# A decoder layer with attention and DeltaNet heads: the second half's x on GpSimd's queue, squares as stationary in the norm sums, a residual that is loaded later

## The chip, the cores and the metric

One core of a Trainium2 chip runs the whole kernel. The metric is the device time of one execution in microseconds (us). The engines are TensorE (PE; its weight loads are PEld), VectorE (DVE), ScalarE (ACT), GpSimd (POOL) and SyncE (SP). SP computes nothing here: it only issues transfers. ACT and POOL issue transfers too, each on a queue of its own, between their own instructions.

## The reference, cut to what matters

One layer, batch 1, 1024 positions, width 1024, all in float32:

```
u    = RMSNorm(x)
proj = u @ w_in            # attn q|k|v, dn q|k|v, dn z gate, dn beta, dn a
A    = sliding-window attention with sinks (8 heads, 2 kv heads, window 128)
qc, kc, vc = silu(causal_conv(dn q|k|v))
qc   = qc * rsqrt(sum(qc*qc) + eps) * 128**-0.5      # l2norm per row and head
kc   = kc * rsqrt(sum(kc*kc) + eps)
B    = chunked gated delta rule over 16 chunks of 64, a scan with a 128x128 state
       per head (4 heads), then a gated RMSNorm
h    = x + concat(A, B) @ w_o
h   += relu(RMSNorm(h) @ w_up)**2 @ w_down
h   += sigmoid(RMSNorm(h) @ w_ple_gate) * (p @ w_ple_proj)
out  = RMSNorm(h)
```

The changed code sits in three places: the loading of x for RMSNorm, the sums of squares for the two l2norms, and the x in `h = x + ...`.

## The kernel before, in words

The positions are worked on in two halves (`hb` 0 and 1) of 512. Every float32 product of a weight is made of three passes of float32r matmuls (high with high, high with low, low with high; `PASSES`), so a weight is loaded, cast on ACT (L219) and its low part subtracted on DVE or POOL (L220) before TensorE can use it. All matmuls have the line L102, the line of a helper, so the names of the tiles say which is which: `bk<-w,U` and `bk<-U,w` are projections of the first half, `bk<-R,w`, `bk<-w,R` those of the second, `bk<-w,AT` the early product `p @ w_ple_proj`, `bk<-vn,ka` a step of the DeltaNet scan, `bk<-rD,wide` a sum of squares. In this trace the second name of a pair is the moving operand in some rows and the stationary in others; the shape at the end of a row is that of the moving side.

The text of the kernel is not the order in which it runs. A class `Flow` runs generators against an invented clock: the DeltaNet and attention chains are tasks that yield times, and the big products (`projections`, `embed`, `w_out`) are a filler that gives TensorE work whenever no task is due. Behind it a scheduler of the framework orders the instructions of each engine by its own model. So an edit in one place can change the order of instructions far from it. On the chip each engine then takes its list in order and waits at an instruction whose inputs are not there, with everything that stands behind it.

The names in the order of time:

- `u_step(hb, ...)` (L347 to L358) loads the eight 128x512 pieces of xT of one half (256 KB each, L351), scales and splits each into high and low parts for the first projection (ACT, DVE), squares it (ACT) and adds it up (`eng`, here POOL, L358). The second half has only four slots (`AT`) for its eight pieces, and the sum `rsb` is the first of them.
- `wunit2` (L278 to L285) loads two k tiles of a weight on SP's queue (L281) into one of two `raw` buffers.
- `scalars`, `norms`, `pre`, `inverse` (L627 to L784) prepare the DeltaNet half: `norms` makes the sums of squares of q and k for each row and head, `pre` the products k*k and k*q with their decay (`ka`, L751) and writes blocks of them to DRAM (`LD`, L757, SP's queue); `inverse` reads them back into `rD` (L770, SP), multiplies (L775, DVE) and solves a small triangular system on DVE (L779, L780).
- `merge`, `prep`, `scan` finish the inverse for each 128 rows and run the recurrent scan.
- `embed` (L1049 to L1079) is spare filler: `p @ w_ple_proj`, copied out of PSUM by ACT (L1072) and stored to DRAM (`PD`, L1075, SP).
- `w_out(hb)` (L1004 to L1045) loads x of that half once more as the residual (L1006, two transfers of 1 MB on ACT's queue, into `H` and for the second half also `AT`), multiplies by w_o and adds on DVE.

Of the kernel before, what the change touches and what calls it, by code (L numbers as in the profile page):

```python
# [12 lines left out]
AF = mybir.ActivationFunctionType  # L13
ALU = mybir.AluOpType
# [4 lines left out]
P = 128  # L19
# [4 lines left out]
HB = 512  # L24
FF = 4096
EPS = 1e-6
# [92 lines left out]
def hybrid_block(ctx, tc, t, out):  # L119
    nc = tc.nc  # L120
    V, A, G, SY = nc.vector, nc.scalar, nc.gpsimd, nc.sync
    flow = Flow()
    T = Pe(tc, flow)
    cnt = [0]

    def nm(s):
        cnt[0] += 1
        return f"{s}{cnt[0]}"
# [13 lines left out]
    def bank(p):  # L142
        return p.tile([P, 512], F32, tag="b", name=nm("bk"))
# [13 lines left out]
    def take(k):  # L157

        live = ring[k]
        while live.n == 0:  # L160
            yield live
        live.n -= 1
        b = bank(ps[k])

        def free():
            live.n += 1
        return b, free

    def ctile(shape, name, dt=F32):
        return cp.tile(shape, dt, tag=name, name=name)  # L170
# [13 lines left out]
    ident = con[:, K_ID:K_ID + P]  # L184
    mle = con[:, K_LE:K_LE + P]
    onesR = ctile([P, P], "ones", F32R)
    ones = onesR.bitcast(F32)
# [56 lines left out]
    def uview(u, b, kt):  # L244
        o = (b * KT + kt) * HB
        return u[:, o:o + HB]
# [31 lines left out]
    def wunit2(src, k2, c0, lo_eng=None, n=256):  # L278

        raw = wraw.tile([P, WN], F32, tag="raw", name=nm("raw"))[:, :2 * n]  # L280
        SY.dma_start(raw.rearrange("p (k n) -> p k n", k=2),  # L281
                     src.rearrange("(k p) n -> p k n", p=P)[:, k2 * 2:k2 * 2 + 2, c0:c0 + n])
        w = wsp.tile([P, 2, WN], F32R, tag="w", name=nm("w"))[:, :, :2 * n]
        split(w[:, 0], w[:, 1], raw, lo_eng or G)
        return w  # L285
# [57 lines left out]
    def slot(n):  # L343
        return AT[n // 4][:, n % 4 * HB:(n % 4 + 1) * HB]


    def u_step(hb, u, eng):  # L347
        def step(kt):
            acc = rsb[hb]
            xr = slot(4 * hb + kt % (4 if hb else 8)) if kt else acc  # L350
            SY.dma_start(xr, t["xT"][kt * P:(kt + 1) * P, hb * HB:(hb + 1) * HB])  # L351
            g = gmix[:, kt:kt + 1]
            A.activation(uview(u, 0, kt), xr, AF.Copy, scale=g)
            V.scalar_tensor_tensor(uview(u, 1, kt), xr, g, uview(u, 0, kt).bitcast(F32),
                                   op0=ALU.mult, op1=ALU.subtract)
            A.activation(xr, xr, AF.Square)
            if kt:
                eng.tensor_tensor(acc, acc, xr, op=ALU.add)  # L358
        return step
# [253 lines left out]
    def dt_(shape, name, p=dn, bufs=None, dt=F32):  # L613
        return p.tile(shape, dt, tag=name, name=nm(name), bufs=bufs)
# [2 lines left out]

    dn0 = zs.rearrange("p t (h s) -> p t h s", h=4)
    dn1 = []

    wide = ctile([P, 2 * P], "wide")
    G.memset(wide, 0.0)
    G.memset(wide[:, P:P + 1], 1.0)
    sel = lambda c: wide[:, P - c:2 * P - c]
    offL = con[:, K_OFF:K_OFF + 64]

    def scalars(s, hb):  # L627
# [42 lines left out]
    def norms(s, q, k):  # L670

        b, free = yield from take("e")
        sq = dt_([P, 2, 4, P], "rD", bufs=1, dt=F32R).bitcast(F32).rearrange("p i h c -> p i (h c)")
        xs = [(sel(h * 32 + i), x[:, h, 3:]) for i, x in enumerate((q, k)) for h in range(4)]
        for j in range(9):
            if j < 8:
                A.activation(sq[:, j % 2], xs[j][1], AF.Square)
                yield 0.99
            if j:
                T.matmul(b, xs[j - 1][0], sq[:, (j - 1) % 2], start=j == 1, stop=j == 8)  # L680
        sb = dt_([P, 4, P], "et", bufs=1).rearrange("p h c -> p (h c)")
        A.copy(sb, b)
        free()
        yield 2.38
        b, free = yield from take("e")
        for tt in range(4):
            T.transpose(b[:, tt * P:(tt + 1) * P], sb[:, tt * P:(tt + 1) * P], ident)
        for i in range(2):
            V.tensor_scalar(s["ss"][:, i].rearrange("p (t h) -> p t h", t=4),
                            b.rearrange("p (t h x) -> p x t h", t=4, h=4)[:, i], EPS, None,  # L690
                            op0=ALU.add)
        free()
        w = lambda name: dt_([P, 16], name, bufs=2)
        rk2, rk, c2d, cc, bb = w("rk2"), w("rk"), w("c2d"), w("cc"), w("bb")
        ssq, ssk = s["ss"][:, 0], s["ss"][:, 1]
        V.reciprocal(rk2, ssk)
        V.tensor_tensor(bb, s["beta"], rk2, op=ALU.mult)
        yield 3.17
        b, free = yield from take("e")
        T.transpose(b[0:16, 0:P], bb, ident)  # L700
        bT = dt_([16, P], "bT", bufs=1)
        A.copy(bT, b[0:16, 0:P])
        free()
        SY.dma_start(s["BD"], bT)
        bS = dt_([P, 32], "bS")
        for x in range(2):
            SY.dma_start(bS[x * 64:x * 64 + 64], s["BD"].rearrange("y (b c) -> (y b) c", b=4))
        G.tensor_tensor(rk, ssk, mhalf, op=ALU.pow)
        sc4 = dt_([P, 4, 2, 2, 2], "sc4", bufs=2)
        v = lambda x: x.rearrange("p (t g h) -> p t g h", t=4, g=2)  # L710
        V.tensor_tensor(sc4[:, :, :, 0], v(bb), v(s["eG"]), op=ALU.mult)
        V.tensor_tensor(sc4[:, :, :, 1], v(s["beta"]), v(rk), op=ALU.mult)
        V.reciprocal(c2d, ssq)
        V.tensor_scalar(c2d, c2d, 1.0 / (128.0 * 128.0), None, op0=ALU.mult)
        G.tensor_tensor(cc, ssq, mhalf, op=ALU.pow)
        V.tensor_scalar(cc, cc, 128.0 ** -0.5, None, op0=ALU.mult)
        s.update(bb=bb, bS=bS, sc4=sc4, c2d=c2d, cc=cc)
# [281 lines left out]
    def hT(hb, j, n=1):  # L999

        x, o = (H, XW + j * HB) if hb == 0 else (H, j * HB) if j < 4 else (AT[1], (j - 4) * HB)
        return x[:, o:o + n * HB]

    def w_out(hb):  # L1004
        for j in (0, 4):
            A.dma_start(hT(hb, j, 4).rearrange("p (j s) -> p j s", j=4),  # L1006
                        t["xT"].rearrange("(j p) s -> p j s", p=P)[:, j:j + 4, hb * HB:hb * HB + HB])

        def rhs(b, kt):
            return dn1[b][:, kt - 4] if hb and kt > 3 else uview(R1, b, kt)  # L1010

        def steps(g, bs, ks):
            for kt in ks:
                if kt % 2 == 0:
                    w = wunit2(t["w_o"], kt // 2, g * 256, (G, G)[hb])
                for m in range(2):
                    o = kt % 2 * 256 + m * P
                    (mm3h, mm3h)[hb](bs[m][0], lambda a: w[:, a, o:o + P], lambda b: rhs(b, kt), kt == 0, kt == KT - 1)
                    if kt < KT - 1 or m == 0:
                        yield  # L1020
            if kt == KT - 1:
                for m in range(2):
                    h = hT(hb, g * 2 + m)
                    V.tensor_tensor(h, bs[m][0], h, op=ALU.add)
                    bs[m][1]()
                yield

        early = ["gg", "ge", "ee"] if hb else []
        held = []
        for g, names in enumerate(early):  # L1030
            if "e" in names:
                yield prepped
            bs = []
            for k in names:
                bs.append((yield from take(k)))
            yield from steps(g, bs, range(4))
            held.append(bs)
        if hb:
            yield pairs_done[1]
        for g in range(4):  # L1040
            if g < len(held):
                yield from steps(g, held[g], range(4, KT))
                continue
            bs = []
            for k in "gg":  # L1045
                bs.append((yield from take(k)))
            yield from steps(g, bs, range(KT))
# [37 lines left out]
    def projections():  # L1085
# [37 lines left out]
        dn1.extend(h4(part(x, F32R)) for x in ("AT0", "Z"))  # L1123
        mixed.done = True
        yield from w_out(0)
        mix_split(1, 0)
        yield from w_out(1)


    b = bank(ps["e"])  # L1130
# [288 lines left out]
    for n in range(16):  # L1419
        q = qs[n].load() if n < 4 else Quad(n).load()  # L1420
# [21 lines left out]
    def bank2():  # L1442
        par[0] = (par[0] + 1) % 8
        return bank(ps["gygygywy"[par[0]]])
# [5 lines left out]
    for c in range(FF // 512):  # L1450
# [13 lines left out]
        for nh in range(2):  # L1464
            wd = []
            for hb in range(2):
# [9 lines left out]
                for m in range(4):  # L1476
                    h = hT(hb, nh * 4 + m)
# [4 lines left out]
    for kt in range(KT):  # L1482
        for nh in range(2):
            i = kt * 2 + nh
# [11 lines left out]
    for tt in range(NT):  # L1496

        nT = mpart().rearrange("p (b k s) -> p b k s", b=2, k=KT)
        hb, ts = tt // 4, slice(tt % 4 * P, tt % 4 * P + P)
        hs_ = [hT(hb, j, 4).rearrange("p (j s) -> p j s", j=4)[:, :, ts] for j in (0, 4)]  # L1500
        hv, c2, cg, c = hn[:, tt % 2 * D:(tt % 2 + 1) * D], ba[:, tt, 0:2], ba[:, tt, 2:3], ba[:, tt, 3:4]
# [3 lines left out]
        for q in range(2):  # L1505
            b = bank2()
# [99 lines left out]
```

## Time and profile before

| | us |
|---|---|
| median of 3 runs | 1371.62 |
| the three runs | 1372.47, 1365.68, 1371.62 |
| the profiled execution's own time | 1366.2 |
| its span in the trace | 1364.1 |
| TensorE busy (share of the span) | 1317.7 (97%) |
| VectorE busy | 838.8 (61%) |
| ScalarE busy | 548.0 (40%) |
| GpSimd busy | 434.5 (32%) |
| mean granted TensorE clock | 0.987 |

The profiled execution is one execution; 2.1 us of its time lie outside the span. Busy time is the time in which an engine works on an instruction; the granted clock is a share of full speed, so a stretch at 0.60 holds fewer columns than its busy time suggests. The kernel's instructions are pipelined on TensorE, so its busy time holds short waits between matmuls as well.

### The profile page before, as it was taken

Reading aid. Unit: us, or ns where it says so; the run is one execution under the profiler, and the core shown is the slowest. Engines: PE = TensorE matmul, PEld = TensorE weight load, DVE = VectorE, ACT = ScalarE, POOL = GpSimd, SP = SyncE. Lnnn points to the kernel's source line nnn. Section 1 sums busy time; section 2 is a strip of 40 time slices with the busy share of each in tenths; the row PEclk is TensorE's granted clock in tenths of the full one; section 3 lists DMA queues with packets and bytes.
Section 4 is the critical chain, followed back from the end, with each engine's and each line's share of the span. In section 5 each row is a group of like instructions: output and inputs, shape, how many; then the busy total and the mean of one; then the engine's idle time right before and its main releaser. Section 6 shows DMA issues by size and latency. Waiting matters only on the chain.

```text
span 1364.1 us, 20392 instructions
## 1 busy us (share of the span) xinstructions
PE 1317.7 (97%) x7664; PEld 1125.5 (83%) x7664; DVE 838.8 (61%) x1558; ACT 548.0 (40%) x1083; POOL 434.5 (32%) x430
## 2 busy tenths in 40 slices
PE   8999999999998999898999999999999999999997
PEld 6788688999897998886788888877888888888886
DVE  6786977697564755797776676654333343344553
ACT  6456375544544433564333333342122231221333
POOL 6673626631385452300011111103122212210332
PEclk9999999999999999999999999999999999999999
DMA  6322222324135431321433323354333333232211
GB/s 223 88 54 73 54 62 52 74 73 105 34 119 176 133 110 33 115 85 63 146 116 116 124 87 114 109 185 136 96 116 101 98 123 120 77 93 73 75 62 47
DMA packets 102738, 134.33 MB, mean 98 GB/s; under 512 B 16400, under 2 KB 71744, under 8 KB 102384
## 3 DMA queue, kind: packets, MB, share of 16 engines
q1 hardware_dynamic: 90528, 110.50, 27.0%
q10 hardware_dynamic: 11760, 21.77, 4.4%
q8 instruction: 60, 0.98, 0.3%
q0 software_dynamic: 352, 0.76, 0.2%
q14 instruction: 38, 0.31, 0.1%
HBM read 106.77 MB, written 26.23 MB: 98 GB/s over the span
## 4 chain that ended last, share of the span: by engine, by line
PE 74%; DVE 11%; DMA 6%; ACT 3%; issue 3%; POOL 2%; SPq 1%; POOLq 0%; ACTq 0%; DVEq 0%
PE bk L102 72%; PE bk L106 2%; DVE w L220 1%; DVE cv L412 1%; DMA AD<-t 1%; ACT w L219 1%; DMA raw<-in_w_in 1%; POOL rsb L358 1%; DMA PD<-po 1%; DMA raw<-in_w_down 1%; DMA H<-in_w_in 1%; DMA AT<-in_xT 0%; DVE gg L649 0%; DMA raw<-AD 0%; SPq L841 0%
## 5 line engine op out<-in xcount | busy, mean ns | idle before, releaser
L102 PE MATMUL bk<-T,w 128*128 128x512 f32 x2304 | 537.9, 392 | 5.7 <-ACT w L219 4.5
L102 PEld LDWEIGHTS bk<-T,w 128*128 128x128 f32 x2304 | 432.8, 188 | 102.6 <-ACT w L219 6.6
L220 POOL TENSOR_TENSOR w<-raw,w 128x512 fp32r<-128x512 f32 x136 | 180.5, 1329 | 621.3 <-ACT w L219 590.2
L219 ACT CAST w<-raw 128x512 fp32r<-128x512 f32 (+1 forms) x280 | 172.6, 620 | 460.8 <-PE bk L102 340.6
L102 PE MATMUL bk<-R,w 128*128 128x256 f32 (+1 forms) x1536 | 240.7, 312 | 1.4 <-ACT w L219 1.4
L102 PEld LDWEIGHTS bk<-R,w 128*128 128x128 f32 x1536 | 210.8, 189 | 22.9 <-issue 2.3
L220 DVE TENSOR_TENSOR w<-raw,w 128x512 fp32r<-128x512 f32 (+1 forms) x144 | 107.5, 748 | 61.1 <-ACT w L219 60.9
L1478 DVE TENSOR_TENSOR H<-bk,H 128x512 f32<-128x512 f32 x96 | 64.6, 690 | 96.0 <-PE bk L102 96.0
L102 PE MATMUL bk<-U,w 128*128 128x512 f32 (+1 forms) x384 | 80.3, 355 | 1.0 <-ACT ba L472 0.6
L102 PEld LDWEIGHTS bk<-U,w 128*128 128x128 f32 x384 | 60.2, 191 | 14.5 <-issue 4.9
L102 PE MATMUL bk<-w,R 128*128 128x256 f32 (+1 forms) x480 | 69.4, 294 | 0.1
L102 PE MATMUL bk<-w,U 128*128 128x256 f32 (+2 forms) x384 | 64.1, 321 | 5.2 <-ACT AT L478 3.2
L102 PE MATMUL bk<-AT,w 128*128 128x256 f32 (+1 forms) x256 | 65.3, 342 | 1.3 <-DVE t L1363 0.8
L102 PEld LDWEIGHTS bk<-w,U 128*128 128x128 f32 x384 | 55.6, 194 | 12.3 <-ACT AT L478 3.4
L102 PEld LDWEIGHTS bk<-w,R 128*128 128x128 f32 x480 | 61.7, 192 | 4.0 <-issue 3.1
L1348 ACT ACTIVATE t<-t 128x512 f32<-128x512 f32 x64 | 40.3, 631 | 39.1 <-DVE t L1347 38.4
L102 PEld LDWEIGHTS bk<-AT,w 128*128 128x128 f32 x256 | 42.8, 191 | 8.3 <-DVE t L1363 1.9
L102 PE MATMUL bk<-R,T 128*128 128x512 f32 (+1 forms) x204 | 48.7, 386 | 0.0
L220 POOL TENSOR_TENSOR T<-ra,T 128x1024 fp32r<-128x1024 f32 x14 | 33.6, 2398 | 46.7 <-ACT T L219 41.0
L102 PE MATMUL bk<-T,T 128*128 128x512 f32 (+1 forms) x204 | 47.0, 379 | 0.0
L555 ACT ACTIVATE s<-s,mx 128x257 f32<-128x257 f32 (+1 forms) x64 | 31.3, 492 | 36.8 <-DVE mx L553 30.2
L102 PEld LDWEIGHTS bk<-T,T 128*128 128x128 f32 x204 | 36.8, 188 | 7.8
(370 smaller groups left out, 1882.1 us busy)
## 6 DMA issues: line engine op xcount, KB each, us to landing
raw<-in_w_in SPq DMA_DIRECT2D x72, 256.0 KB, 2.8
raw<-in_w_up SPq DMA_DIRECT2D x32, 512.0 KB, 4.9
AD<-t ACTq DMA_DIRECT2D x64, 256.0 KB, 2.7
raw<-in_w_down SPq DMA_DIRECT2D x64, 256.0 KB, 3.0
ra<-AD SPq DMA_DIRECT2D x28, 512.0 KB, 4.1
raw<-in_w_o SPq DMA_DIRECT2D x32, 256.0 KB, 3.1
PD<-po SPq DMA_DIRECT2D x16, 256.0 KB, 3.7
rawg<-in_w_gate SPq DMA_DIRECT2D x16, 256.0 KB, 3.2
```

Of the source, the lines that this page charges most:

```text
L102: self.tc.nc.tensor.matmul(o, lh, rh, **k)
L106: self.tc.nc.tensor.transpose(o, x, i)
L219: A.copy(hi, src)
L220: lo_eng.tensor_tensor(lo, src, hi.bitcast(F32), op=ALU.subtract)
L358: eng.tensor_tensor(acc, acc, xr, op=ALU.add)
L412: V.scalar_tensor_tensor(cv if i < 3 else x[:, 3:], x[:, i:i + HB], cw[:, j, i:i + 1], cv, op0=ALU.mult, op1=ALU.add)
L555: A.activation(s[:, i, lo:257], s[:, i, lo:257], AF.Exp, bias=mx[:, i:i + 1], accum_out=sm[:, i:i + 1])
L1348: A.activation(r, r, AF.Square)
L1478: V.tensor_tensor(h, bs[m], h, op=ALU.add)
```

## The change

It has three parts.

The eight x pieces of the second half are issued by POOL (`G`) instead of SP (`SY`), in the same loop.

In `norms`, the sum over the 128 channels of a head used a 128x128 window of the tile `wide` as stationary (zeros but for one column of ones, so that each of eight matmuls fills one row of a PSUM bank) and the squares, 512 columns, as moving. ACT copied the bank out, four transposes turned it into a second bank, and two DVE instructions added eps. Now each 128x128 block of the squares is the stationary and a column of ones is moving, 32 matmuls of one column for each half; the sums come out with rows on partitions, and one DVE instruction adds eps. `wide` and its two memsets on POOL go.

In `w_out`, the two residual transfers of the second half are issued with j=4 (into `AT`) first. In front of them stands a copy on ACT that reads the first columns of `hT(0,1)` and writes the place where j=0 of the second half will land; `hT(0,1)` is a part of `H` that the first half's residual addition writes.

```diff
@@ u_step
-            SY.dma_start(xr, t["xT"][kt * P:(kt + 1) * P, hb * HB:(hb + 1) * HB])
+            (G if hb else SY).dma_start(xr, t["xT"][kt * P:(kt + 1) * P, hb * HB:(hb + 1) * HB])
@@ before scalars
-    wide = ctile([P, 2 * P], "wide")
-    G.memset(wide, 0.0)
-    G.memset(wide[:, P:P + 1], 1.0)
-    sel = lambda c: wide[:, P - c:2 * P - c]
@@ norms
-        xs = [(sel(h * 32 + i), x[:, h, 3:]) for i, x in enumerate((q, k)) for h in range(4)]
+        xs = [x[:, h, 3:] for x in (q, k) for h in range(4)]
         for j in range(9):
             if j < 8:
-                A.activation(sq[:, j % 2], xs[j][1], AF.Square)
+                A.activation(sq[:, j % 2], xs[j], AF.Square)
                 yield 0.99
             if j:
-                T.matmul(b, xs[j - 1][0], sq[:, (j - 1) % 2], start=j == 1, stop=j == 8)
-        sb = dt_([P, 4, P], "et", bufs=1).rearrange("p h c -> p (h c)")
-        A.copy(sb, b)
-        free()
-        yield 2.38
-        b, free = yield from take("e")
-        for tt in range(4):
-            T.transpose(b[:, tt * P:(tt + 1) * P], sb[:, tt * P:(tt + 1) * P], ident)
-        for i in range(2):
-            V.tensor_scalar(s["ss"][:, i].rearrange("p (t h) -> p t h", t=4),
-                            b.rearrange("p (t h x) -> p x t h", t=4, h=4)[:, i], EPS, None,
-                            op0=ALU.add)
+                i, h = divmod(j - 1, 4)
+                for tt in range(4):
+                    c = i * 16 + tt * 4 + h
+                    T.matmul(b[:, c:c + 1], sq[:, (j - 1) % 2, tt * P:(tt + 1) * P], ones[:, 0:1],
+                             start=True, stop=True)
+        V.tensor_scalar(s["ss"].rearrange("p i x -> p (i x)"), b[:, 0:32], EPS, None, op0=ALU.add)
         free()
@@ w_out
+    def x_in(hb, j):
+        A.dma_start(hT(hb, j, 4).rearrange("p (j s) -> p j s", j=4),
+                    t["xT"].rearrange("(j p) s -> p j s", p=P)[:, j:j + 4, hb * HB:hb * HB + HB])
+
     def w_out(hb):
-        for j in (0, 4):
-            A.dma_start(hT(hb, j, 4).rearrange("p (j s) -> p j s", j=4),
-                        t["xT"].rearrange("(j p) s -> p j s", p=P)[:, j:j + 4, hb * HB:hb * HB + HB])
+        if hb:
+            A.copy(hT(1, 0)[:, 0:8], hT(0, 1)[:, 0:8])
+        for j in (4, 0)[::1 - 2 * (hb == 0)]:
+            x_in(hb, j)
```

Because the scheduler sees other instructions, the order changes far from these lines as well. Three places follow. First SP's list in the first 110 us, before (`rsb` and `AT` are the slots of x, `raw` the weights' buffers):

```order
L281 DMA raw_326<-in_w_in 128x2x264
L281 DMA raw_358<-in_w_in 128x2x264
L351 DMA rsb<-in_xT 128x512
L351 DMA AT_78<-in_xT 128x512 x3
L281 DMA raw_396<-in_w_in 128x2x264
L351 DMA AT_78<-in_xT 128x512
L281 DMA raw_431<-in_w_in 128x2x264
L351 DMA AT_78<-in_xT 128x512
L281 DMA raw_478<-in_w_in 128x2x256
```

And the same part of SP's list after:

```order
L281 DMA raw_323<-in_w_in 128x2x264
L281 DMA raw_355<-in_w_in 128x2x264
L281 DMA raw_393<-in_w_in 128x2x264
L281 DMA raw_428<-in_w_in 128x2x264
L281 DMA raw_475<-in_w_in 128x2x256
L281 DMA raw_528<-in_w_in 128x2x256
```

On SP no x stands between the weights any more; the later rows of both lists are weights as well.

The x pieces now stand in POOL's list, between the additions of the squares. After (the line numbers are one higher; `rsb_129` is the first half's sum, `rsb` the second's; the transfer of the second half's first piece stands much further up, before all of these):

```order
L359 TENSOR_TENSOR rsb_129<-rsb_129,AT_78 128x512 x2
L352 DMA AT_78<-in_xT 128x512
L404 COPY H<-halo 128x3
L359 TENSOR_TENSOR rsb_129<-rsb_129,AT_78 128x512
L352 DMA AT_78<-in_xT 128x512
L359 TENSOR_TENSOR rsb_129<-rsb_129,AT_78 128x512
L352 DMA AT_78<-in_xT 128x512 x2
L359 TENSOR_TENSOR rsb<-rsb,AT_78 128x512
L352 DMA AT_78<-in_xT 128x512
L371 TENSOR_TENSOR rstd<-ms_371,mhalf 128x4
L359 TENSOR_TENSOR rsb<-rsb,AT_78 128x512 x2
L352 DMA AT_78<-in_xT 128x512
```

Each piece is issued by POOL right behind the addition that frees its slot; three more such pairs follow, the last two additions behind the first rotary instructions.

The third place is far from the edits, around 400 to 450 us: DVE's list where the second half's inverse begins (`rD`, `tp`) and the first half's scan ends (`St`, `oS`, `oss`, `vn`). Before:

```order
L934 SCALAR_TENSOR_TENSOR St_3391<-St_3391,ex_546,bk_4665 128x128 x2
L937 TENSOR_TENSOR oS_4606<-bk_4665,oS_4606 128x256
L910 SCALAR_TENSOR_TENSOR vn_4839<-bk_4834,sc_4247,u_4820 128x128 x2
L942 TENSOR_TENSOR oss_4673<-oss_4673,c2d_2143 128x2
L943 TENSOR_SCALAR oss_4673<-oss_4673 128x2
L945 TENSOR_TENSOR oss_4673<-oss_4673,cc_2144 128x2
L949 SCALAR_TENSOR_TENSOR oS_4606<-oS_4606,oss_4673,Z_79 128x128 x2
L775 TENSOR_TENSOR rD_4981<-rD_4981,bS_4243 128x1024
L779 TENSOR_TENSOR tp_4991<-rD_4981,bk_4988 128x31
L780 TENSOR_TENSOR bk_4988<-bk_4988,tp_4991 128x31
```

After (L766 is the former L775, L770 and L771 the former L779 and L780, L940 the former L949):

```order
L766 TENSOR_TENSOR rD_4961<-rD_4961,bS_4157 128x1024
L940 SCALAR_TENSOR_TENSOR oS_4546<-oS_4546,oss_4624,Z_79 128x128 x2
L770 TENSOR_TENSOR tp_4971<-rD_4961,bk_4968 128x31
L771 TENSOR_TENSOR bk_4968<-bk_4968,tp_4971 128x31
L770 TENSOR_TENSOR tp_4974<-rD_4961,bk_4968 128x60
L852 TENSOR_TENSOR kd_5125<-bk_5118,ex_3544 128x256
L771 TENSOR_TENSOR bk_4968<-bk_4968,tp_4974 128x2x30
L925 SCALAR_TENSOR_TENSOR St_3444<-St_3444,ex_543,bk_4732 128x128 x2
L928 TENSOR_TENSOR oS_4664<-bk_4732,oS_4664 128x256
```

Before, L775 stands behind the last row of the first half's scan; after, L766 stands in front of scan steps that are still to be done, and the steps of the triangular solve lie between them. On SP, at the same place, the four weight loads of the second half's w_proj stood in front of the last `LD` store and the `rD` load; now they stand behind both.

## Rows read from the trace of the kernel before

**Rows 1.** windows; busy us (instructions) of PE, PEld, DVE, ACT, POOL; PEclk, DMA share, GB/s.

```profile
24.00:50.00 26.00, 21.28 (x133) 19.31 (x132) 17.40 (x20) 16.28 (x36) 17.03 (x16) 0.93 0.42 115
...
400.00:450.00 50.00, 41.19 (x299) 39.70 (x298) 26.48 (x64) 22.62 (x60) 28.82 (x28) 0.86 0.57 174
...
525.00:556.00 31.00, 24.47 (x194) 22.74 (x193) 16.76 (x55) 13.01 (x47) 8.61 (x10) 0.96 0.11 35
```

**Rows 2.** windows, same columns, 5 us stretches inside the 400 to 450 us stage.

```profile
405.00:410.00 5.00, 3.70 (x19) 3.70 (x20) 4.64 (x10) 1.12 (x3) 2.45 (x3) 0.69 0.37 97
...
435.00:440.00 5.00, 4.16 (x34) 3.78 (x32) 1.66 (x6) 0.39 (x2) 2.01 (x2) 1.00 1.05 367
...
440.00:445.00 5.00, 1.63 (x7) 1.63 (x8) 0.76 (x5) 2.90 (x8) 2.10 (x3) 0.60 0.65 190
...
445.00:450.00 5.00, 5.00 (x34) 5.00 (x33) 4.69 (x12) 1.86 (x5) 1.10 (x1) 0.71 0.78 235
```

**Rows 3.** PE timeline: start, us, line, operation, count; in brackets idle before, releaser.

```profile
406.30 1.56 PE L102 MATMUL bk<-xk 128*128 128x128 f32 x8 [2.03 <-DVE ka L751]
...
420.19 0.92 PE L102 MATMUL bk<-vn,ka 128*128 128x128 f32 x4 [2.52 <-ACT oS L913]
...
443.37 5.10 PE L102 MATMUL bk<-w,AT 128*128 128x256 f32 x24 [3.77 <-ACT po L1072]
```

**Rows 4.** chain of waits, 400 to 460 us: start, us, what.

```profile
432.57 10.09 DMA PD<-po
```

**Rows 5.** timeline of ACT's DMA queue, 425 to 440 us.

```profile
430.07 0.98 ACTq L1006 DMA_DIRECT2D H<-in_xT  x2
```

**Rows 6.** DMA issues: out<-in, queue, count, KB each, median us to landing.

```profile
PD<-po SPq DMA_DIRECT2D x16, 256.0 KB, 3.7
...
H<-in_xT ACTq DMA_DIRECT2D x3, 1024.0 KB, 7.1
...
AT<-in_xT SPq DMA_DIRECT2D x14, 256.0 KB, 4.1
...
tab<-in_rope POOLq DMA_DIRECT2D x1, 256.0 KB, 7.4
```

**Rows 7.** timeline of SP's DMA queue, 0 to 110 us.

```profile
34.98 1.74 SPq L351 DMA_DIRECT2D AT<-in_xT  x2
...
44.43 62.26 SPq L281 DMA_DIRECT2D raw<-in_w_in  x17
```

**Rows 8.** PE timeline, 36 to 70 us.

```profile
44.46 3.08 PE L102 MATMUL bk<-w,U 128*128 128x264 f32 x23 [0.89 <-DVE w L220]
...
48.64 11.86 PE L102 MATMUL bk<-U,w 128*128 128x512 f32 x50 [0.63 <-ACT ba L472]
```

**Rows 9.** PE timeline around one of the row-selecting matmuls of norms, first half.

```profile
187.38 1.02 PE L102 MATMUL bk<-rD,wide 128*128 128x512 f32 x2
...
187.84 0.68 PE L102 MATMUL bk<-kH,qT 128*128 128x256 f32 x1
...
188.36 0.28 PE L102 MATMUL bk<-kL,qT 128*128 128x256 f32 x1
```

**Rows 10.** PE timeline: column sums of four tiles, what follows, and four transposes.

```profile
29.35 0.95 PE L102 MATMUL bk<-ones,rsb 128*128 128x1 f32 x8
...
30.16 0.61 PE L102 MATMUL bk<-w,U 128*128 128x264 f32 x3
...
201.04 0.60 PE L106 MATMUL bk<-con,et 128*128 128x128 f32 x4
```

**Rows 11.** POOL timeline: one DMA issue, and two adds of L358.

```profile
4.66 0.54 POOL L451 DMA_DIRECT2D tab<-in_rope  x1
...
24.95 1.80 POOL L358 TENSOR_TENSOR rsb<-rsb,AT 128x512 f32<-128x512 f32 x1
```

**Rows 12.** DVE timeline: last L751 of the second half, and L775.

```profile
431.05 0.68 DVE L751 TENSOR_TENSOR ka<-bk,et 128x512 f32<-128x512 f32 x1
...
446.69 1.22 DVE L775 TENSOR_TENSOR rD<-rD,bS 128x1024 f32<-128x1024 f32 x1
```


## The prediction

> **What bounds the kernel now.** I read the busy table first: TensorE is busy for 97% of the span, no other engine above 61%. So time is lost only where TensorE waits, works at a lower granted clock, or does work that can go. The windows by stage show where it waits. In [rows 1] the first value is the length, the second TensorE's busy time, PEclk the granted clock. From 24 to 50 us 4.7 of 26 us are idle at clock 0.93. From 400 to 450, where the first half's scan ends and the second half's inverse begins, 8.8 of 50 are idle at 0.86: (1 - 0.86) x 50 = 7.0 more, 15.8 in all. From 525 to 556, the second half's scan, 31 - 24.5 = 6.5 idle and 0.04 x 31 = 1.2 by the clock. Behind that the changed code doesn't run.
>
> I then took the 400 to 450 stage in steps of 5 us. In [rows 2] the clock is 0.69, 0.60 and 0.71 in the poorest ones, each near or behind TensorE's shortest busy times, and DMA moves 367 GB/s from 435 to 440. TensorE's timeline names the waits: in [rows 3] 2.03 us for `ka` from DVE, 2.52 for the scan's `oS`, and 3.77 for `po`, ACT's copy in the spare filler. That copy needs a buffer which a store to `PD` must leave first; the chain of waits has that store at 10.09 us [rows 4]. At 430.07 ACT's queue has issued two residual transfers at once [rows 5]. These are 1 MB each, and a `PD` store has a median of 3.7 us against its 10.09 here [rows 6]. So the burst of residual loads makes the store late, the store makes the copy late, the copy starves the filler.
>
> At the start I read SP's queue. Two x pieces go at 34.98, and the next weight load stands in the queue until 44.43 [rows 7], behind x pieces whose slots are not free. TensorE's timeline has a wait of 0.89 and one of 0.63 there [rows 8]: little, since the waits of that stretch are many and small.
>
> **Part by part: the norm sums.** A selecting matmul starts at 187.38 and the next matmul at 187.84; that one takes 0.68 instead of the 0.28 of its like [rows 9]. So each costs 0.46 + 0.40 = 0.86 us, and 2 x 8 of them 13.8. Four transposes take at most 0.60 [rows 10], for two halves 1.2. What comes in, 2 x 32 float32 matmuls of one column, the kernel does already in `u_rstd`: four of them start at 29.35 and the next work at 30.16 [rows 10], so 0.20 each, 64 x 0.203 = 13.0. Net: 13.0 - 15.0 = -2.0. The range is -3 to +1, since the four may be hidden a little better or worse among other work. The ACT copy and the second DVE addition lie on engines that idle more than half of the time; I take 0 for them, and the shorter chain of the norms as part of the order below.
>
> There is a rule that would make this part far better. In the rows, four such sums have eight records and 0.81 us, 0.10 each. The Trainium skill, "TensorE: Matmul & The Clock Gate", section "Back-to-back issue gap", puts matmuls of 1 to 64 columns at about 25 ns each; by that the 128 added records would cost 3.2 us and the part would give -11.8. The section says as well that in a stream of weight load and matmul both set the spacing, and here each record loads 128 columns of weights for one that moves, as the 0.10 of the row shows. I hold by the row.
>
> **The x loads.** SP's queue no longer holds weights behind x, and the 0.89 + 0.63 = 1.5 us can go. Against it: POOL issues now, at 0.54 us for an issue [rows 11], 8 x 0.54 = 4.3 us, beside additions of 1.80 each. POOL is busy 17.0 of 26 us in that stretch [rows 1], so 9.0 are free and 4.3 fit. A transfer on POOL's queue took 7.4 us to land, on SP's 4.1 [rows 6]; 3.3 later for a piece. Weights are two buffers ahead, but x pieces follow one another through four slots, so a piece that is 3.3 late can be seen. If one piece in four is, TensorE gets 2 x 3.3 = 6.6 late at worst, of which the cover takes half. I take -1.0, with -1.5 to +3 as ends. It lies nearer the lower, because the second half's x fills its slots while TensorE still has first-half projections (the `bk<-w,U` of rows 8) before it.
>
> On this the Trainium skill has a rule against the change: "SBUF — State Buffer", section "SBUF: two separate sides" says that DVE instructions using both ports keep POOL from writing descriptors, so that its transfers start late. The additions of [rows 11] do take 1.80 us while DVE is busy, which would fit it, but no row shows a POOL transfer in such a moment. By the rule the loads are late by up to a long DVE instruction, which lies within the +3.
>
> **The residual.** Of the 15.8 us lost from 400 to 450, this is what I tie to the burst: the wait of 3.77, and the clock of 0.60 and 0.71 in the two stretches from 440 to 450, (0.40 + 0.29) x 5 = 3.45 us; sum 7.2. With the load of j=0 held back by the copy behind the first half's residual addition, and j=4 alone at first, half of the burst goes; I take -6. The other waits (2.03 and 2.52 in rows 3, the clock of 0.69) sum to the remaining 8.6. Here the new order counts: about a hundred matmuls of the second half's projections, and more of the spare filler, come later and fill this stage, so I take -4 of it. What is late next is the inverse: SP now has the last `LD` store and the `rD` load in front of the w_proj weights, and DVE has its multiplication in front of remaining scan steps. I put +2 on it. Sum -8; ends: -15.8 (nothing is lost) and +12 (the rival A below, without the other terms).
>
> Between the copy and the load that waits for it, ACT's own work queues behind the copy: if the first half's residual addition is late, ACT stands. By then only the product with w_o remains, which needs weight casts from ACT; two weights ahead cover that.
>
> **The end of the scan.** From 525 to 556 7.8 us are lost, and more filler is there. I take half, -4; from -7.8 to +3, as the load of j=0 now lands in it (7.1 us for 1 MB in rows 6, ahead of a residual addition that is late in each product).
>
> **Everything else.** From 50 to 400 us the order is written anew with the same work. I take 0, with 4 either way: 350 us at a busy share that was nearly full has little to give.
>
> **Sum.** -2.0 - 1.0 - 8 - 4 = -15.0 against the profiled execution of 1366.2 us (its span is 1364.1, 2.1 lie outside it), which gives 1351.2. The median before is 1371.62, 5.4 above the profiled one; the three runs lie within 6.8 of one another, and I don't know which part of that the changed kernel keeps. With three quarters of it I get 1355.
>
> **Rivals.** A, slower: DVE and SP take their lists in order. The last `ka` was made at 431.05 and its multiplication came at 446.69, 15.6 us later [rows 12]; the stores and loads through DRAM lie between. If the new multiplication again waits 15.6 us, now with scan steps behind it on DVE and w_proj loads behind the `LD` store on SP, the scan and the filler both stop: 15.6 idle and as much clock as the 5 us stretches show, 0.34 x 5 = 1.7. With the gains of the norms and the start, -3, and the residual's -6 used up by it: 15.6 + 1.7 - 3 - 6 = +8, and without the residual's gain +14. From 1366.2 + 8, with the same share of the median's offset, it is 1378; with +14 1384. It decides if that wait is not filled by the scan work ahead of it. Against it: much of the 15.6 was DVE's place in the order, since the scan stood in front.
>
> B, no change: the burst moves to a later place and slows a store or weight there, and the other waits stay: -2 -1 +0 to 4, so 1363 to 1367, and 1367 to 1371 with the offset.
>
> C, more: all of 15.8 and 7.8 goes, with -3: -26.6, or 1339.6, with the offset 1343.6. The norms at the -11.8 that the Trainium skill's issue gap gives (in "TensorE: Matmul & The Clock Gate") would bring the forecast to 1345; against the row it has 0.03, in these 0.13.
>
> D, the held-back load is hidden anyway and x on POOL is late: +3 at the start, -4 in the tail, norms -2: 1363, with the offset near 1367. It goes with B.
>
> **How the numbers follow.** Forecast 0.54; A 0.11; B with D 0.22; C 0.13. A run of this kernel can tell 0.5% from no change, which is 6.9 us: faster is below 1364.8, slower above 1378.5. Faster holds all of the forecast (0.54) and of C (0.13) and a fifth of B (0.05), 0.72; the same holds the rest of B (0.17) and a part of A (0.02), 0.19; slower 0.09. The range: the forecast's own is 1348 to 1362, the stage's ends being far apart; with B it reaches to 1370 and with C down to 1343, which leaves about 0.2 out.
>
> **What would show it.** Right: the granted clock from 400 to 450 above 0.93, no wait of more than 2 us for `po`, the `PD` stores at their median, one residual transfer at a time, the start's weight loads on SP without a hold of several us, 64 one-column sums at 0.2 us. Wrong: TensorE waiting for DVE's inverse (`rD`, `tp`) or for the scan's `vn` behind it; a projection waiting for an x piece from POOL; the 15.8 us found again at a later place.

## The result, and the profile after

The changed kernel is slower: 1381.27 us (median of 8 runs, 1372.51 to 1387.51) against 1367.97 before (8 runs, 1365.68 to 1372.47). The ratio is 1.0092, with an interval of 1.0071 to 1.0113. The forecast was 1355, range 1343 to 1370. The profiled execution took 1380.95 us, 14.8 more than the one of before; TensorE is busy for 1328.4 us, 10.7 more, and its mean granted clock fell from 0.987 to 0.980. Over the two spans that is (1 - 0.980) x 1379.1 - (1 - 0.987) x 1364.1 = 9.9 us of clock, so nearly all of the added busy time; the other 4.3 us of the longer span are idle. Over all eight runs the mean clock is 0.982, against 0.987 to 0.988 for the kernel before in its later rounds: some 7.6 us of about 13. So the clock carries the larger part of the loss, not all of it.

Windows of the kernel after, in the columns of [rows 1] (length, then the busy time of PE, PEld, DVE, ACT and POOL, then PEclk, DMA share, GB/s):

```profile
24.00:50.00 26.00, 23.57 (x142) 21.08 (x140) 15.85 (x19) 14.64 (x28) 17.93 (x19) 0.93 0.43 123
...
355.00:390.00 35.00, 34.73 (x253) 33.81 (x254) 13.38 (x40) 13.88 (x30) 11.99 (x9) 0.71 0.10 31
...
400.00:450.00 50.00, 42.09 (x328) 40.33 (x327) 30.98 (x77) 24.55 (x60) 28.98 (x29) 0.88 0.45 134
450.00:525.00 75.00, 71.13 (x692) 68.24 (x692) 47.07 (x121) 29.72 (x67) 35.83 (x32) 0.97 0.42 129
525.00:556.00 31.00, 31.00 (x274) 30.61 (x273) 14.94 (x42) 14.42 (x43) 11.81 (x11) 1.00 0.25 80
```

And two of these stretches before, which the prediction had not looked at:

```profile
355.00:390.00 35.00, 35.00 (x302) 29.71 (x301) 18.07 (x58) 16.41 (x43) 19.13 (x14) 1.00 0.13 38
...
450.00:525.00 75.00, 75.00 (x754) 72.22 (x753) 47.78 (x124) 27.79 (x62) 35.40 (x30) 1.00 0.33 96
```

The row to see is 355 to 390. TensorE is busy nearly all the time in both kernels (34.73 and 35.00 of 35 us), so a look at waits finds little; but the clock is 0.71 instead of 1.00, and the row counts 253 matmul records instead of 302. That is 0.29 x 35 = 10.2 us. The stage of the forecast's largest term, 400 to 450, lost 15.8 before and loses 7.9 + 0.12 x 50 = 13.9 now, a gain of 1.9 instead of 8. From 450 to 525 nothing was lost before; now it is 3.9 + 0.03 x 75 = 6.1. The tail's gain is 7.8 in its old window, yet the scan now ends later: its last step on DVE starts at 573.8 instead of 557.2.

What stands in the slow stretch, on TensorE's timeline of the kernel after (start, us, operation, count):

```profile
362.27 1.40 PE L102 MATMUL bk<-ones,rD 128*128 128x1 f32 x12
363.60 0.68 PE L102 MATMUL bk<-XT,ka 64*64 64x64 f32 x16
...
369.87 2.29 PE L102 MATMUL bk<-ones,rD 128*128 128x1 f32 x10
...
372.34 2.69 PE L102 MATMUL bk<-w,R 128*128 128x256 f32 x11
```

These are the second half's one-column sums, the 64-column merges and few projections. At full clock 12 records of the sums take 1.40 us, 0.12 each; at the lower clock 10 take 2.29, 0.23 each. Not the whole stretch is behind the sums: from 355 to 360 the clock is already 0.66, behind a wait of 1.64 us for `X` and almost ahead of the first of them. That is 1.7 of the 10.2 us. From 360 to 365 it is 1.00, and from 365 on it falls again with no wait in front of it.

The rows that answer to [rows 3] and [rows 12], at 440 us: DVE's timeline first, then TensorE's.

```profile
435.33 0.42 DVE L846 TENSOR_TENSOR u<-bk,sc 128x256 f32<-128x256 f32 x1
440.06 1.23 DVE L766 TENSOR_TENSOR rD<-rD,bS 128x1024 f32<-128x1024 f32 x1 [4.32 <-issue]
441.20 0.61 DVE L940 SCALAR_TENSOR_TENSOR oS<-oS,oss,Z 128x128 f32<-128x128 f32 x2
```

```profile
441.61 0.48 PE L106 MATMUL bk<-con,oS 128*128 128x128 f32 x1 [5.04 <-DVE oS L940]
```

DVE stands 4.32 us at L766, which waits for the `LD` round trip through DRAM (the load into `rD` is issued at 435.30); L940, a step of the scan that could run, stands behind it, and TensorE waits 5.04 us for it. That is the place of rival A, at a third of its price.

The rows that answer to [rows 8], and the new wait of the stretch from 450 to 525, on TensorE's timeline after:

```profile
10.97 22.34 PE L102 MATMUL bk<-w,U 128*128 128x512 f32 x92 [2.69 <-ACT w L219]
44.69 4.59 PE L102 MATMUL bk<-w,U 128*128 128x264 f32 x23 [2.17 <-DVE w L220]
...
491.45 0.68 PE L102 MATMUL bk<-XT,ka 64*64 64x64 f32 x16 [2.44 <-DVE XT L793]
```

The wait for a weight at 44 us is 2.17, longer than the 0.89 of before, not gone. The `PD` stores did get faster, 2.9 us in place of the 3.7 of [rows 6], on the page's table of DMA issues:

```profile
PD<-po SPq DMA_DIRECT2D x16, 256.0 KB, 2.9
```

### The profile page after: what moved, and what is told of

The parts are those of the page before. It is cut to its first block, busy times and chain, and to the rows that moved or that the text cites. A ratio compares the mean times of both kernels' runs of the same rounds, so it can differ in the third digit from the quotient of the medians.

```text
span 1379.1 us, 20546 instructions
## 1 busy us (share of the span) xinstructions
PE 1328.4 (96%) x7752; PEld 1142.4 (83%) x7752; DVE 836.2 (61%) x1556; ACT 551.0 (40%) x1084; POOL 441.5 (32%) x436
## 4 chain that ended last, share of the span: by engine, by line
PE 70%; DVE 9%; DMA 8%; ACT 4%; issue 4%; POOL 3%; SPq 1%; POOLq 0%; ACTq 0%; DVEq 0%
PE bk L102 68%; PE bk L106 2%; DMA raw<-in_w_o 2%; DMA raw<-in_w_in 2%; DVE w L220 2%; POOL w L220 1%; ACT w L219 1%; DMA raw<-in_w_down 1%; DVE cv L413 1%; DMA AD<-t 1%; DMA H<-in_w_in 1%; POOL rsb L359 1%; DVE gg L645 0%; DMA Xt<-XD 0%; DVE t L1344 0%
## 5 line engine op out<-in xcount | busy, mean ns | idle before, releaser
L220 POOL TENSOR_TENSOR w<-raw,w 128x512 fp32r<-128x512 f32 x136 | 182.7, 1345 | 640.3 <-ACT w L219 573.5
L102 PE MATMUL bk<-R,w 128*128 128x256 f32 (+1 forms) x1536 | 246.5, 315 | 3.7 <-ACT w L219 2.7
L102 PEld LDWEIGHTS bk<-R,w 128*128 128x128 f32 x1536 | 214.4, 191 | 26.2 <-ACT w L219 4.0
L220 DVE TENSOR_TENSOR w<-raw,w 128x512 fp32r<-128x512 f32 (+1 forms) x144 | 107.9, 751 | 62.6 <-ACT w L219 62.3
L102 PE MATMUL bk<-U,w 128*128 128x512 f32 (+1 forms) x384 | 76.9, 346 | 1.7 <-DVE w L220 1.2
L220 POOL TENSOR_TENSOR T<-ra,T 128x1024 fp32r<-128x1024 f32 x14 | 33.5, 2395 | 45.4 <-ACT T L219 39.4
```

The source lines that it names most:

```text
L102: self.tc.nc.tensor.matmul(o, lh, rh, **k)
L220: lo_eng.tensor_tensor(lo, src, hi.bitcast(F32), op=ALU.subtract)
```

## The experiments

Theory 1: the second half's one-column sums lower TensorE's granted clock, some 10 us. Its rival: the sums are as cheap as forecast, and the rewritten order costs the time. Every kernel was timed beside the kernel before; ratios are to that, with their 95% intervals in brackets.

**One part at a time.** e1 takes only the norm sums, e3 only POOL's loads, e4 only the residual, e2 the two without the sums; each has the other parts as before.

> Only the norm sums are changed; x loads and residual as before. Theory 1 (the 64 one-column sums lower TensorE's granted clock where little else lies between them, 0.50 to 0.84 from 365 to 390 us in the changed kernel, some 10 us): 1374 to 1380, and stretches at 0.50 to 0.84 around the second half's sums. Rival (the sums are as cheap as forecast and the time is lost by the rewritten order and the x loads): 1362 to 1368, clock 1.00 around the sums.

> The changed kernel with the norm sums of before (wide selector). Theory 1: the clock stays at 1.00 around the second half's sums and the time falls by about 10 from the changed kernel's 1381, to 1368 to 1373. Rival: it stays near 1378 to 1383.

> Only the second half's x goes to POOL's queue. Theory 2 (the piece for rsb is issued at 5.77 us and shares the transfers with the first half's first pieces, whose second piece lands 2.4 us later: the first long wait is 2.7 instead of 0.9): first projection starts at about 11.0 instead of 9.0 us, time 1370 to 1373. Rival (the later start is made good by 100 us): 1366 to 1369.

> Only the residual loads are changed. If the burst of two 1 MB loads is what starved the filler from 440 to 450 us, the time is 1360 to 1365 and no wait for po of over 2 us is left; if the waits only move, 1366 to 1370; if the copy that holds j=0 back stops ACT, over 1372.

| | median us | ratio |
|---|---|---|
| e1 norm sums only | 1374.25 | 1.0068 [1.0046, 1.0089] |
| e2 x and residual | 1369.85 | 1.0025 [1.0010, 1.0040] |
| e3 x only | 1367.09 | 1.0011 [0.9995, 1.0027] |
| e4 residual only | 1370.06 | 1.0023 [1.0009, 1.0037] |

The parts add up within their intervals: 0.68 + 0.25 = 0.93% against 0.92% for the whole. No part made the kernel faster. The sums are three quarters of the loss, and in e1 the low clock stands at the same place as in the changed kernel. e3's second group of projections starts at 9.42 us, while that of e1, whose x is still on SP's queue, starts at 10.75; so the late start of the changed kernel (10.97) doesn't come from x on POOL, and my theory 2 falls. x on POOL's queue can't be told from no change.

e4's profile shows where the gain of the burst's end was lost again. TensorE's timeline of e4, the two places:

```profile
440.90 1.93 PE L102 MATMUL bk<-w,AT 128*128 128x256 f32 x12 [2.03 <-ACT po L1078]
...
489.30 0.68 PE L102 MATMUL bk<-XT,ka 64*64 64x64 f32 x16 [2.66 <-DVE XT L802]
```

DVE's timeline at the second place, before and then in e4:

```profile
486.31 0.45 DVE L802 STREAM_TRANSPOSE XT<-Xt 128x256 f32<-128x256 f32 x1 [1.83 <-DMA Xt<-XD]
486.68 1.45 DVE L1247 TENSOR_TENSOR rsb<-rsb,t 128x512 f32<-128x512 f32 x2
```

```profile
487.56 1.33 DVE L1253 TENSOR_TENSOR rsb<-rsb,t 128x512 f32<-128x512 f32 x1 [5.00 <-ACT t L1251]
488.82 0.43 DVE L802 STREAM_TRANSPOSE XT<-Xt 128x256 f32<-128x256 f32 x1
```

And e4's windows at 440, 485 and 550 us:

```profile
440.00:445.00 5.00, 4.10 (x24) 4.10 (x25) 1.38 (x4) 3.22 (x9) 2.55 (x2) 0.72 0.92 267
445.00:450.00 5.00, 5.00 (x42) 5.00 (x42) 4.58 (x21) 1.69 (x3) 2.00 (x2) 0.94 0.51 171
485.00:490.00 5.00, 2.34 (x31) 2.08 (x30) 2.44 (x3) 3.22 (x6) 2.63 (x3) 1.00 0.30 63
490.00:495.00 5.00, 5.00 (x41) 4.87 (x42) 1.24 (x3) 1.66 (x3) 5.00 (x6) 0.66 0.31 100
...
550.00:555.00 5.00, 2.95 (x15) 2.35 (x15) 2.54 (x9) 1.74 (x7) 0.76 (x2) 0.64 0.03 10
555.00:560.00 5.00, 4.22 (x20) 3.85 (x20) 1.95 (x6) 1.80 (x7) 0.63 (x1) 0.50 0.00 0
560.00:565.00 5.00, 5.00 (x38) 5.00 (x38) 1.40 (x6) 1.32 (x3) 1.83 (x2) 0.84 0.00 0
```

At 440 the forecast's mechanism works: the wait for `po` goes from 3.77 to 2.03 and the clock loss from 3.45 to (0.28 + 0.06) x 5 = 1.7, a gain of 3.5. At 489 it is paid back: the first `XT` (L802) now stands on DVE behind an addition of the MLP's squares that waits 5.00 us for ACT, while before the first `XT` came ahead of that addition; TensorE waits 2.66 and then works at 0.66, 1.7 more. The clock at 550 to 565 costs another (0.36 + 0.50 + 0.16) x 5 = 5.1, where before the same three windows had 0.87, 0.79 and 1.00 and cost 1.7. The order of the two loads moves nothing: on ACT's queue j=0 still goes before the load into `AT` in e4 (460.89 and 496.05 us) and in the changed kernel (480.87 and 528.02), as before the change (430.07 and 495.64). What changed is that the copy holds j=0 back. This is one profile for each kernel; no run takes the later losses apart from one another.

**How many columns a sum moves.** The sums of e1 with 2, 4, 8 and 16 columns of ones; in e6 the moving operand is a 128-column window of zeros with a single column of ones, and the sums of a half add up in one block. e5's edit:

```diff
-                    T.matmul(b[:, c:c + 1], sq[:, (j - 1) % 2, tt * P:(tt + 1) * P], ones[:, 0:1],
+                    T.matmul(b[:, c * 16:c * 16 + 16], sq[:, (j - 1) % 2, tt * P:(tt + 1) * P], ones[:, 0:16],
...
-        V.tensor_scalar(s["ss"].rearrange("p i x -> p (i x)"), b[:, 0:32], EPS, None, op0=ALU.add)
+        V.tensor_scalar(s["ss"].rearrange("p i x -> p (i x)"), b.rearrange("p (c x) -> p c x", x=16)[:, :, 0], EPS, None, op0=ALU.add)
```

> The norms-only kernel, but each of the 64 sums moves 16 columns of ones in place of 1. Theory 1 (too few moving columns lower the granted clock in the second half's sums): the clock there stays partly low or recovers, time between 1366 and 1374. Rival (the rewritten order is the cause): 1372 to 1376 and the clock around the sums as in the norms-only kernel.

> The norms-only kernel, but the 32 sums of a half move 128 columns, a window of zeros with one column of ones, and add up in one block of PSUM; the squares are still the stationary. Theory 1: clock 1.00 around the sums and 1363 to 1368 (each sum 0.21 to 0.30 us in place of 0.20). Rival (order): 1372 to 1378 with a low clock at the same place.

> The norms-only kernel with 2 moved columns for each sum; every engine has the order of the 1-column form. Columns theory: still 20 us or so at low clock between 355 and 386 us and 1372 to 1376, since 2 is hardly more than 1. Order theory: the same. A time under 1368 would say that the 1-column form is a case by itself.

> 4 moved columns, another order behind the sums, the same as that of 8 columns. Columns theory: still some 14 to 24 us at low clock between 355 and 386 us, 1369 to 1375. Order theory (the 1-column form's order is the cause): as with 16 columns, 1361 to 1366.

> 8 moved columns, the order of the 4-column form on every engine. Columns theory: less low clock than with 4 columns, by 3 us of time or more, 1363 to 1370. Order theory: the time of the 4-column form within 1.5 us.

| columns | median us (range) | ratio | mean granted clock over the runs |
|---|---|---|---|
| 1 (e1) | 1374.25 (1372.36 to 1379.01) | 1.0068 [1.0046, 1.0089] | 0.983 |
| 2 (e13) | 1372.98 (1363.93 to 1382.39) | 1.0059 [1.0036, 1.0082] | 0.985 |
| 4 (e14) | 1369.67 (1361.95 to 1376.98) | 1.0032 [1.0011, 1.0052] | 0.983 |
| 8 (e15) | 1366.20 (1359.40 to 1376.10) | 1.0012 [0.9991, 1.0032] | 0.986 |
| 16 (e5) | 1363.18 (1359.93 to 1367.10) | 0.9986 [0.9973, 0.9999] | 0.990 |
| 128 (e6) | 1368.85 (1363.80 to 1371.44) | 1.0028 [1.0014, 1.0041] | 0.987 |

From 1 to 16 the time falls with each step, though neighbouring intervals overlap; the mean clock doesn't rise with each (0.983 with 4 as with 1). e5 came out below both ranges that I had named for it. e13 has e1's instructions in e1's order on every engine, and shows what the clock costs: its runs go from 1363.93 at a mean clock of 0.990 to 1382.39 at 0.976, and its profiled execution is the one at 0.990. The same rows in e1 and in e13, on TensorE's timeline; first e1:

```profile
369.84 2.29 PE L102 MATMUL bk<-ones,rD 128*128 128x1 f32 x10
...
386.55 0.27 PE L106 MATMUL bk<-con,bb 128*16 128x128 f32 x1
```

then e13:

```profile
363.86 1.28 PE L102 MATMUL bk<-ones,rD 128*128 128x2 f32 x10
...
374.77 0.27 PE L106 MATMUL bk<-con,bb 128*16 128x128 f32 x1
```

and the window from 370 to 375 in e1 and in e13:

```profile
370.00:375.00 5.00, 5.00 (x24) 5.00 (x25) 2.09 (x5) 2.14 (x4) 0.06 (x1) 0.50 0.00 0
```

```profile
370.00:375.00 5.00, 5.00 (x48) 4.75 (x47) 3.37 (x10) 0.47 (x2) 2.54 (x3) 1.00 0.09 32
```

From these sums to the transpose of `bb` e1 needs 16.7 us and e13 10.9: equal instructions, 24 against 48 matmul records in 5 us. Over the stretch from `X` in front of it (353.29 and 350.91) it is 33.3 against 23.9, 9.4 us for the clock alone. It doesn't show that two columns keep the clock up where one doesn't: e13's slowest run is slower than any of e1's, and by their medians the two can't be told apart. 4 and 8 columns also have one order between them; 1369.67 against 1366.20, and 0.983 against 0.986 in the clock, go the way of the columns, but the intervals of the time overlap. The forms with 4 and more columns stand in other orders than e1, so the step from 2 to 4, which brings no clock, and that from 8 to 16 are not columns alone; e6, with no low clock from 350 to 430, loses at 436 and 480 us (waits of 5.52 and 3.99).

**Where the sums stand, and with how much between them.** e7 has the new sums in the first half alone; e8 yields 2.5 instead of 0.99 us of the invented clock between two groups.

> The new sums in the first half alone, the wide selector kept in the second. Theory 1 (where enough projection work lies between the sums the clock holds, and they are as cheap as forecast): 1363 to 1367. Rival (the sums cost by themselves, wherever they stand): 1369 to 1371, half of the norms-only loss.

> The norms-only kernel with the sums spread: the task yields 2.5 us of the invented clock between two groups of sums instead of 0.99, so more projection work stands between them. Theory 1: fewer stretches at 0.50 around the second half's sums, 1366 to 1371. Rival (the order elsewhere or the sums themselves): 1373 or more.

e7 missed both ranges: 1377.45, 1.0089 [1.0073, 1.0106]. e8 missed that of theory 1 and fell into the rival's: 1379.42, 1.0099 [1.0081, 1.0118]. In e7's profile the sums of the first half cost nothing by the clock: from 160 to 400 us it is 1.00. That profile is also the control for the second half. Up to the first of the second half's norm sums, at 356.88 us in e7 and 358.12 in e1, TensorE takes the same list of matmuls in both, with the same wait in front (1.77 and 1.76 us for `X`). Behind that e7 has the selecting matmuls of before and e1 the one-column sums. e7's window beside the one of e1 above:

```profile
370.00:375.00 5.00, 5.00 (x35) 3.69 (x34) 0.46 (x2) 1.81 (x4) 4.08 (x5) 1.00 0.17 52
```

From 355 to 390 us the clock is 1.00 in all six profiles whose second half has no sums of 16 columns or fewer (before, e2, e3, e4, e6 and e7; e6 and e7 have orders of their own). It is 0.66 to 0.79 in the four with one column (the changed kernel, e1, e8 and e10) and 0.85 to 0.99 in the seven with 2 to 16. So the low clock goes with these sums and not with one order; why it falls in some executions and not in others of the same program stays open.

e7's time was lost elsewhere. Its windows at the end of the first scan:

```profile
440.00:445.00 5.00, 4.07 (x16) 3.08 (x14) 4.40 (x14) 3.36 (x9) 2.76 (x3) 0.50 0.58 213
445.00:450.00 5.00, 2.19 (x10) 1.90 (x11) 4.83 (x12) 0.62 (x1) 2.92 (x3) 0.50 0.30 100
```

e8 kept the low clock, only later (0.50 from 380 to 395), and its chain ran behind: the second half's last `ka` at 446.9 instead of 428.1 in e1. A longer yield didn't bring more filler to the place: between 376 and 397 us 13 records of projections stand there.

**The whole change with 16 columns, and the scan in front.** e9 is the changed kernel with e5's edit. e10 to e12 put one tiny DVE instruction in front of the inverse, for the changed kernel, for e5 and for e9:

```diff
+        if s is s01[1]:
+            yield pairs_done[0]
+            V.scalar_tensor_tensor(s["bS"][:, 0:2], zs[:, 3, 0:512:256], 0.0, s["bS"][:, 0:2],
+                                   op0=ALU.mult, op1=ALU.add)
```

> The whole change, but each sum moves 16 columns in place of 1. If the one-column sums cost some 10 us by the clock, the changed kernel's 1381 becomes 1368 to 1373 and the clock from 360 to 390 us is 1.00. If the norms-only result does not carry over to the whole change, it stays at 1376 to 1382.

> The whole change with its one-column sums, and one tiny DVE instruction (it adds zero times two outputs of the first half's scan to bS) that makes the inverse's multiplication wait for the end of the first half's scan, so that on DVE it stands behind all of that scan's steps, as before the change. Theory (DVE stands at the multiplication for its transfer from 435 to 440 us with scan steps behind it, which cost TensorE a wait of 5.04 and most of a stretch at low clock): the wait for oS goes, 1372 to 1377. Rival (the wait only moves to the later inverse): 1379 to 1384.

> Norms only, 16 columns, and the same tiny instruction in front of the inverse. If the 5.76 us wait behind the multiplication and the low clock after it go, 1356 to 1361, the fastest so far; if the later inverse makes the second half's scan late, 1363 to 1367.

> The whole change with 16 columns and the tiny instruction in front of the inverse: with both losses gone 1361 to 1367; what is left against the norms-only version of it is what the x loads and the residual cost, about 3 us as the two alone measured.

e9: 1365.08, 1.0015 [0.9995, 1.0035]. One edit of the moved columns takes the changed kernel from 1.0092 to no difference, though it brings another order too; the mean clock over the runs rises from 0.982 to 0.989, some 9.6 us. Its range is wide (1361.41 to 1376.18), and its profiled execution, one of the slower, still has a low clock at 373 to 384 us.

e10 to e12: 1385.29, 1372.50 and 1372.87, ratios 1.0146 [1.0126, 1.0166], 1.0055 [1.0041, 1.0069] and 1.0064 [1.0045, 1.0083]. By these ratios each is 0.5 to 0.7% slower than its like without the instruction, 7 to 9 us, and above every range that I had named. In e10 the wait of 5.04 us is gone (none from 425 to 470 us is longer than 1.73), so there the rival holds: the wait at L766 cost less than the late inverse. In e11 and e12 it was only replaced, by 4.00 and 3.54 us in e11 and 3.90 in e12, so these two test less. In e11 the solve ends 20.75 us later than in e5; ACT's copies of its result, first e5, then e11:

```profile
468.19 0.59 ACT L771 COPY et<-bk 128x512 f32<-128x512 f32 x1
```

```profile
488.94 0.58 ACT L775 COPY et<-bk 128x512 f32<-128x512 f32 x1
```

The second half's scan then ends with less other work beside it. Windows of its last part, again e5 and e11:

```profile
540.00:570.00 30.00, 29.09 (x246) 28.68 (x245) 16.31 (x34) 14.96 (x38) 12.51 (x11) 1.00 0.35 113
```

```profile
540.00:570.00 30.00, 24.47 (x168) 22.52 (x168) 13.56 (x40) 10.36 (x36) 8.26 (x9) 0.83 0.11 36
```

e11 idles 5.5 of 30 us where e5 idles 0.9, and works at 0.83 in place of 1.00.

## Why the prediction was wrong

The forecast was a sum of -15 us; the change measured +0.92%, some 13 us. Two steps of the sum failed. The norm sums, put at -2.0, measured +0.68% (e1), 9.3 us. The stage from 400 to 450 and the tail, put at -8 and -4, gave nothing: without the sums the change is still 0.25%, 3.4 us, slower (e2).

**The norm sums: the step that made the loss.** At full clock the prices were about right: 0.20 to 0.24 us for a sum (0.12 for a record, two records a sum), and in e7 two selecting matmuls take 1.81 us up to the start of the next (356.88 to 358.69), 0.90 each against the 0.86 forecast. A net of -2.0 is not shown by any run. What the step left out is that its durations came from [rows 9] and [rows 10], all read where the clock was 1.00, among projections. The second half's sums stand between 64-column merges with few projections, and there the clock fell: 10.2 us in the changed kernel's profile, of which 1.7 stand ahead of the sums. The prediction followed the clock in [rows 2] only behind waits, and had no rival in which busy work lowers it. The rule that it weighed (the Trainium skill, "TensorE: Matmul & The Clock Gate", section "Back-to-back issue gap") puts such a matmul by itself at about 25 ns; the rows have 0.12 us at full clock, so the measurement decides. That was not the question that decided the time.

**The x loads.** -1.0 was forecast; e3 gives +1.5 with an interval that takes in no change. The weight load at 44.43 us in [rows 7] was not held behind x pieces, as the prediction read it: the last of them had been issued at 36.39, and the load waited 7.6 us for DVE's L220 to free its buffer. With no x on SP's queue it goes at 44.67 in the changed kernel and at 43.31 in e3. The waits of that stretch were not many and small either; the 4.7 us are three, of which this one, ahead of [rows 8], is the largest:

```profile
33.98 9.59 PE L102 MATMUL bk<-w,U 128*128 128x264 f32 x64 [3.20 <-ACT AT L478]
```

In e3 it is 1.82; the 0.89 stayed (0.85), and the 0.63 at 48.64 became 1.84. Nor did POOL's transfers come late by 3.3 us: the seven into `AT` have a median of 3.6 us in e3, not the 7.4 of the one in [rows 6].

**The residual.** The wait for `po` and the clock behind it did follow the burst, but the sum was wrong. The burst's end gave 3.5 of the 6, and the "+2" for what is late next was too little: L802 behind the squares and the low clock at 490 and 550 took 2.66 + 1.7 + 3.4 back in e4's profile. e4 measured +0.23%. Two readings were off besides: the other waits and the clock that the prediction names come to 2.03 + 2.52 + 0.31 x 5 = 6.1, not the 8.6 that it drew -4 from; and the load that lands from 525 to 556 is that into `AT` (528.02), not j=0 (480.87).

**400 to 450 and the tail.** Rival A's wait came, 5.04 us instead of 15.6. It was not what decided: e10, which takes it away, is slower still. I had given rival A 0.11; the time fell into its range (1378 to 1384) for a reason that none of the cases held, which is luck and not a hit. The new order was to give -4 in the stage and -4 in the tail; the stage gained 1.9 in the profile, and the tail's 7.8 were outweighed by the 6.1 lost from 450 to 525 and by 4.5 from 556 to 600 (2.7 idle, 0.04 x 44 by the clock; 0.4 in all before). Why the same stage costs 13.9 us under an order so different was not settled beyond these waits.

## What to carry to other kernels

A matmul swapped for ones that move few columns is to be priced at both clock levels: look at what lies beside it in each place where it runs, not at the one row that shows it among dense work. A busy TensorE in a window says nothing by itself; read the granted clock and the count of matmuls beside it. And where a scheduler writes the order, time each edit alone: here a single edit (e7) cost 0.9% in a place far from it.

## What the runs showed that I had not expected

Moving 16 columns of the same ones, fifteen of them thrown away, is faster than moving 1: e5 is 11 us faster than e1 (with another order behind the sums), and with 0.9986 [0.9973, 0.9999] the only one of sixteen versions that beat the kernel before, and so barely that it may be chance. One program in one order ran between 1363.93 and 1382.39 us (e13), as its mean granted clock went from 0.990 to 0.976. A small DVE dependence meant to restore the former order cost 0.5 to 0.7% in three kernels.
